# Five more seven-product pairs in the down projections, and earlier DMA sums, in a two-layer fp32 encoder on one core

## The chip, the cores and the metric

The kernel runs on one core of a Trainium2 chip. The metric is the time of one execution on the device in microseconds (us), and the median over several runs is compared. In the views of the profile PE is the tensor engine (PEld its weight loads), DVE the vector engine, ACT the scalar engine, POOL the GpSimd engine and SP the engine that issues most of the DMA transfers.

## The reference: what is computed

Two layers over 256 tokens of width 2048. Each layer has an input projection, a token mixer (differential attention in layer 0, windowed attention in layer 1) beside four memory heads, an output projection, and then an MLP with 8192 hidden features. Nearly all the work is matrix products with weights in fp32. The part that the change is about is this:

```python
x = x + heads @ w_out[i]
h = rms_norm(x, norm_mlp[i])
x = x + jnp.square(jax.nn.relu(h @ w_up[i])) @ w_down[i]
```

## The kernel before

**Numbers.** PE multiplies in a reduced fp32 format, so each fp32 operand is split into a high part and a rest: ACT copies the high part (`split`, line 439, operation CAST), DVE subtracts it to get the rest (line 440, TENSOR_TENSOR). A product is then three matmuls, hi x hi, lo x hi, hi x lo (`three`, lines 531 to 533). Weights come in pieces of 128x1024 fp32 (512 KB). SP issues the loads, at most a few pieces ahead of PE, since there are four buffers for `hi`, four for `lo`, and few for the raw pieces.

**Stages.** In each layer PE does, in this order: input projection ("in": 80 pieces in layer 0, 48 in layer 1), memory keys and values ("mem"), output projection ("out"), `up` (eight column groups of 16 pieces) and `down` (two halves of 32 pairs of pieces, each half 1024 of the 2048 output columns). In `up`, the finished hidden features are transposed on PE (line 1018), passed through relu and square on ACT (lines 1020 and 1021) and kept in `blk` tiles, some of them in DRAM (`hid`, line 1024). The transposes of the last group come when `down` has begun or is about to.

**Seven products instead of eight.** A pair of pieces is a 2 x 2 block problem with eight products, that is 24 matmuls of 512 columns. A "seven-product" or fast pair (`seven`, line 548) does it with seven products, 21 matmuls, in the manner of Strassen and Winograd: it needs sums of the weight blocks and differences of the hidden blocks. The sums are made by `sum_pair`: a first sum `a`, two further sums on DVE (lines 357 and 358), and the splits of `a` (parts `ah`, `al`) and of `b` (`bh`, `bl`). In the traces these four are tiles called `x` or `blk`, written from `big`. `FAST` names the fast pairs of a half of `down`, `LATE` those of layer 0's second half; `LATE_BLK` says which of these keep their sums in `blk`.

**First sums by DMA.** For a fast pair of `down` the first sum can be made in DRAM: POOL issues a copy (line 291) and then an accumulating copy (line 295) into a `madesum` tensor, which SP later loads instead of DVE adding. `make_sums` sets a list of moments, counted in pieces that PE's program has taken up: a first moment (`SUM_AT`), then one step every `SUM_GAP` pieces, or every `SUM_GAP_UP` pieces in `up`. What is left when `up` ends is issued at once (`while making`). Each step issues one addition and the next copy.

**Kept differences.** The hidden differences of a fast pair are made once in `up` (`keep`), split, stored to DRAM by POOL (`kept`, line 1000), and loaded again by POOL for each half, two pairs ahead (`load_kept`, line 1109, into `h2` tiles; there are six of these). Those of the last hidden features are made when `down` has begun.

**What sets the order.** Every engine takes its instructions strictly as the program has them. The order comes from the order of the calls, from `fetch`, which issues loads and splits two or three pieces ahead, and from small tasks that wait for a number of steps. `load_pair(..., early)` asks for a fast pair's raw pieces `LOOK` pairs ahead when enough of six big slots (five quads of the tile `big` and one `blk`) are free. The output projection does not do that before the change. Raw memory features are loaded when they are needed (`mem_part`).

Of the kernel before, what the change touches and what calls it, by code (L numbers as in the profile page):

```python
# [14 lines left out]
F32 = mybir.dt.float32  # L15
# [7 lines left out]
P = 128  # L23
S = 256
# [22 lines left out]
SINGLE = 4  # L47
AHEAD = 2
WARM = 10
FAST = (2, 4, 6, 8, 10, 12, 14, 16, 18, 20, 22, 24, 26, 28, 29)  # L50
LATE = (2, 4, 6, 8, 10, 12, 14, 16, 18, 20, 22, 24, 26, 28)
AWAY = range(6, 15)
LATE_BLK = (8, 12, 16, 20, 24, 28)
LOOK = 2
KEEP_AFTER = (2, 5, 8, 11)
SUM_AT = {0: 20, 1: 2}
SUM_GAP = 4
SUM_GAP_UP = 8
LAM_INIT = 0.8 - 0.6 * math.exp(-0.3 * 0)

G_ATTN, G_MEM, G_MLP = 0, 2 * KT, 4 * KT
# [9 lines left out]
def trunk(ctx: ExitStack, tc: tile.TileContext, xin, xtok, memin, memtok, posrel, gcol, rows,  # L71
# [19 lines left out]
    def quad(tag, shape=(P, 2, 2, 256), dt=F32R):  # L91
        return xp.tile(list(shape), dt, tag=tag, name=nm(tag), bufs={"x2": 8, "h2": 6, "blk": 10}[tag])
# [146 lines left out]
    def fast_pairs(name, h):  # L239

        if name.startswith("out"):
            return OUT_FAST[h]
        if name.startswith("up"):
            return UP_FAST[h]
        if name.startswith("down"):
            return LATE if (name, h) == ("down0", 1) else FAST
        return ()
# [37 lines left out]
    def make_sums(layer):  # L285

        name = f"down{layer}"

        def copy(h, j):
            made_in[name, h, j] = dp.tile([P, 2, 512], F32, name=nm("madesum"))  # L290
            after_piece(nc.gpsimd.dma_start(made_in[name, h, j].rearrange("p a n -> p (a n)"), weights[name][h, 2 * j]))

        def add(h, j):
            upper = weights[name][h, 2 * j + 1][:, 512:1024]
            nc.gpsimd.dma_start(made_in[name, h, j], upper.unsqueeze(1).broadcast_to([P, 2, 512]), accum_op=ALU.add)

        def after_piece(ins):
            tc.add_manual_dep(ins.ins, splits[0], mybir.DependencyInfo(mybir.DependencyClass.Sync, mybir.DependencyReason.DATA),
                              reason="behind a piece")

        def step(i):
            if i:
                add(*wanted[i - 1])
            if i < len(wanted):
                copy(*wanted[i])

        wanted = [(h, j) for h in range(2) for j in fast_pairs(name, h)]
        first, quiet, up = [at_piece[k, layer] for k in ("in", "mem", "up")]
        at = first + SUM_AT[layer]
        for i in range(len(wanted) + 1):  # L310
            making.append((at, lambda i=i: step(i)))
            at += SUM_GAP if at < quiet else SUM_GAP_UP
            at = max(at, up) if at >= quiet else at

    making = deque()
    fetched = [0]
# [11 lines left out]
    def load_pair(name, c, p, early=False):  # L328

        key = (name, c, p)  # L330
        if key in loaded or key in taken_raw or p not in fast_pairs(name, c) or early and len(slots) < (2 if name.startswith("up") else 4):
            return
        src = weights[name][c]
        taken = []
        first = raw_quad(name, (P, 1024), taken)
        nc.sync.dma_start(first, src[2 * p])
        if key in made_in:
            a = raw_quad(name, (P, 2, 512), taken)
            nc.sync.dma_start(a, made_in[key])
            raw = t2k([P, 512])  # L340
            nc.sync.dma_start(raw, src[2 * p + 1][:, 0:512])
        else:
            a = None
            raw = raw_quad(name, (P, 1024), taken)
            nc.sync.dma_start(raw, src[2 * p + 1])
        loaded[key] = first, raw, a, taken
# [23 lines left out]
    def fetch(parts=1, lead=None):  # L370

        name, c, j = plan.popleft()
        src = weights[name][c, j]
        p = j // 2
        seven_ = p in fast_pairs(name, c)
        down = name.startswith("down")
        if seven_:
            load_pair(name, c, p)
            raw = taken_raw[name, c, p][j % 2] if (name, c, p) in taken_raw else loaded[name, c, p][j % 2]
            if j % 2 == 0:  # L380
                taken_raw[name, c, p] = loaded[name, c, p][:2]
        else:
            raw = wp.tile([P, 1024], F32, tag="raw", name=nm("raw"))
        if name.startswith(("up", "down")) and j % 2 == 0:
            if down:
                load_hidden(p)
            for i in range(1, LOOK + 1):
                load_pair(name, c, p + i, True)
            if down:
                load_hidden(p + 1)  # L390
        hi = wp.tile([P, 1024], F32R, tag="hi", name=nm("hi"))
        lo = wp.tile([P, 1024], F32R, tag="lo", name=nm("lo"))
        n = 1024 // parts
        if seven_:
            with tc.issue_after(done[0].ins):
                if j % 2 == 0:
                    if down:
                        taken = sum_pair(name, c, p)
                    split(hi, lo, raw)
                else:  # L400
                    split(hi[:, 0:512], lo[:, 0:512], raw[:, 0:512])
                    if not down:
                        taken = sum_pair(name, c, p)
                    slots.extend(held_slots.pop(name, []) if down else taken)
                if down and j % 2 == 0:
                    held_slots[name] = taken
        else:
            for i in range(parts):
                s = slice(i * n, (i + 1) * n)
                if lead is not None:  # L410
                    lead(i)
                behind[0] = nc.sync.dma_start(raw[:, s], src[:, s])
                done[0] = split(hi[:, s], lo[:, s], raw[:, s])
                splits.append(done[0].ins.name)
        ready.append(((name, c, j), hi, lo))
# [64 lines left out]
    def chunk_tok(w, c, X2, before=None, lead=None, steps=1):  # L480
        ps = [bank("mm") for _ in range(2)]
        for j in range(8):
            if before is not None:
                before(j)
            hi, lo = piece(w, c, j, lead and (lambda i: lead(2 * j + i)))
            for kk in range(2):
                for t in range(2):
                    k = 2 * j + kk
                    ws = slice(kk * 512, kk * 512 + 512)
                    xh = X2[k][:, 0, t * P:(t + 1) * P]  # L490
                    xl = X2[k][:, 1, t * P:(t + 1) * P]
                    nc.tensor.matmul(ps[t], lhsT=xh, rhs=hi[:, ws], start=(k == 0), stop=False)  # L492
                    nc.tensor.matmul(ps[t], lhsT=xh, rhs=lo[:, ws], start=False, stop=False)  # L493
                    nc.tensor.matmul(ps[t], lhsT=xl, rhs=hi[:, ws], start=False, stop=(k == KT - 1))  # L494
            tick(steps)
        return ps
# [384 lines left out]
    def mem_stats():  # L881
# [22 lines left out]
                              parts[-1:], wait=MEM_AT, gap=0))  # L904
        Task([Light(means, 0)], parts)

    def mem_part(layer, qm, qd, H2):
        M2 = Halves()
        box = {}

        def before(j):
            if j % 2 == 0:
                raw = quad("h2", (P, 4, S), F32)
                nc.sync.dma_start(raw, memin[:, 512 * j:512 * j + 1024].rearrange("p (k s) -> p k s", s=S))
                box["raw"] = raw
            for k in (2 * j, 2 * j + 1):
                src = box["raw"][:, k % 4, :]
                make_x2(M2, k, src, gc[:, G_MEM + layer * KT + k:G_MEM + layer * KT + k + 1])

        ps = chunk_tok(f"mem{layer}", 0, M2, before)  # L920
        kT, kd = norm_T(ps, mst, 4, gc[:, G_MK + layer:G_MK + layer + 1], layer == 0)
        vbox = [None, None]
        heads = [plain_head(h, h, qm, kT, vbox, None, None, H2, 12 + h) for h in range(4)]
        firsts = [Task(h[:1], (qd, kd)) for h in heads]
        ps = chunk_tok(f"mem{layer}", 1, M2)
        flush([kd])
        vbox[0], vbox[1] = val_split(ps, mst)
        for i, h in enumerate(heads):
            done_heads[12 + i] = Task(h[1:], [firsts[i]])
# [256 lines left out]
    for g in range(3):  # L1186
# [20 lines left out]
        kT, kd = norm_T(ps, st0, 8, gc[:, G_AK:G_AK + 1])  # L1207
        for h in range(4):
            done_heads[4 * g + h] = Task(diff_head(h, qT, kT, v, bias, H2, 4 * g + h), [qd, kd] + rows_done)
    ps = chunk_tok("a", 9, X2)  # L1210
    qm, qd = norm_T(ps, st0, 4, gs[:, 2:3])
    mem_part(0, qm, qd, H2)
    X2 = out_proj(0, H2)
# [12 lines left out]
    for g in range(3):  # L1226
        ps = chunk_tok("b", g, X2)
        qT, qd = norm_T(ps, st1, 4, gs[:, 1:2])
        for h in range(4):
            n = 4 * g + h  # L1230
            done_heads[n] = Task(plain_head(h, n // 3, qT, kT, vv, bias, rw[:, R_SINK + n:R_SINK + n + 1], H2, n), [qd, kd])
    ps = chunk_tok("b", 5, X2)
    qm, qd = norm_T(ps, st1, 4, gs[:, 3:4])
    mem_part(1, qm, qd, H2)
    X2 = out_proj(1, H2)
# [70 lines left out]
```

## Time and profile before

| what | value |
|---|---|
| median of 3 runs (lowest, highest) | 2082.97 us (2082.69, 2083.38) |
| the profiled execution | 2082.35 us |
| its span | 2080.6 us |
| PE busy in the span | 2071.5 us |
| DVE busy | 1769.7 us (85%) |
| ACT busy | 1266.7 us (61%) |
| POOL busy | 182.1 us (9%) |
| moved by DMA | 563.62 MB, 271 GB/s on average |

On PE's clock of the trace, layer 0's `up` runs from 416 to 762 us, the halves of `down` from 762 to 929 and from 929 to 1096. In layer 1 `up` runs from 1396 to 1742, and `down` to 1913 and to 2081. A timeline row gives the start, the duration, the engine, the line, the operation with output and inputs, and in brackets the idle time before it with what ended it. A row of windows gives for each stretch the busy time of PE, PEld, DVE, ACT and POOL, then the granted PE clock (1.00 is full speed), the busy share of the DMA engines and what they moved. Matmuls overlap, so a matmul's listed duration is longer than the distance to the next.

### The profile page before, as it was taken

How to read it: one execution, taken by the hardware profiler on the slowest of the kernel's cores; microseconds unless marked ns; L12 is line 12 of the kernel's file. 1: busy time of each engine (PE TensorE's matmuls, PEld its weight loads, DVE VectorE, ACT ScalarE, POOL GpSimd, SP SyncE). 2: the span in 40 equal slices, each digit the busy share in tenths (PEclk: the TensorE clock that was granted, in tenths of full speed). 3: DMA queues.
4: the chain of work that ended last, by engine and by line, in shares of the span. 5: the costliest groups of instructions: out<-in, count | busy, mean ns of one | idle time of the engine just before them, and what ended most of it. 6: DMA issues, size and time to landing. Idle time of an engine off the chain costs nothing. (4 is left out here: it accounts for less than half of the span.)

```text
span 2080.6 us, 28646 instructions
## 1 busy us (share of the span) xinstructions
PE 2071.5 (100%) x10011; PEld 1720.7 (83%) x10011; DVE 1769.7 (85%) x2545; ACT 1266.7 (61%) x1892; POOL 182.1 (9%) x286
## 2 busy tenths in 40 slices
PE   9999999999999999999999999999999999999999
PEld 7878888888888888888888888888888887888887
DVE  7667778898999998898886677889999988989888
ACT  7467665566555666667655566566555665666664
POOL 1311100000011110000001100000001111000000
PEclk9999999999999999999999999999999999999999
DMA  8898864588899889988979975567789999998894
GB/s 319 298 297 273 270 204 158 188 257 242 266 292 295 262 287 333 335 282 285 332 259 291 269 233 194 172 211 239 251 276 292 295 280 338 323 334 311 289 334 167
DMA packets 168000, 563.62 MB, mean 271 GB/s; under 512 B 19456, under 2 KB 20480, under 8 KB 166656
## 3 DMA queue, kind: packets, MB, share of 16 engines
q1 hardware_dynamic: 132544, 439.62, 61.0%
q0 software_dynamic: 35168, 122.18, 21.8%
q8 instruction: 78, 1.28, 0.2%
q14 instruction: 66, 0.54, 0.1%
q10 hardware_dynamic: 144, 0.01, 0.0%
HBM read 531.19 MB, written 92.41 MB: 300 GB/s over the span
## 5 line engine op out<-in xcount | busy, mean ns | idle before, releaser
L439 ACT CAST hi<-raw 128x1024 fp32r<-128x1024 f32 (+1 forms) x522 | 525.6, 1036 | 443.6 <-issue 133.5
L440 DVE TENSOR_TENSOR lo<-raw,hi 128x1024 fp32r<-128x1024 f32 (+1 forms) x522 | 617.3, 1206 | 195.2 <-ACT hi L439 193.8
L492 PE MATMUL mm<-hi,x 128*128 128x512 f32 x640 | 255.8, 402 | 0.6 <-ACT hi L439 0.6
L493 PE MATMUL mm<-lo,x 128*128 128x512 f32 x640 | 250.7, 392 | 0.2 <-DVE lo L440 0.2
L494 PE MATMUL mm<-hi,x 128*128 128x512 f32 x640 | 250.2, 391 | 0.2 <-DVE x L436 0.2
L439 ACT CAST h<-big 128x1024 fp32r<-128x1024 f32 (+1 forms) x100 | 101.7, 1020 | 149.5 <-DVE big L283 130.8
L532 PE MATMUL mm<-lo,h 128*128 128x512 f32 (+1 forms) x461 | 179.2, 389 | 1.3 <-DVE lo L440 1.3
L531 PE MATMUL mm<-hi,h 128*128 128x512 f32 (+1 forms) x461 | 179.0, 389 | 1.4 <-ACT hi L439 1.4
L533 PE MATMUL mm<-hi,h 128*128 128x512 f32 (+1 forms) x461 | 178.9, 388 | 0.0
L532 PE MATMUL aux<-lo,h 128*128 128x512 f32 x442 | 172.2, 390 | 0.2 <-DVE lo L440 0.2
L531 PE MATMUL aux<-hi,h 128*128 128x512 f32 x442 | 172.2, 390 | 0.0
L533 PE MATMUL aux<-hi,h 128*128 128x512 f32 x442 | 172.0, 389 | 0.0
L531 PE MATMUL mm<-hi,x 128*128 128x512 f32 x414 | 161.7, 391 | 0.0
L533 PE MATMUL mm<-hi,x 128*128 128x512 f32 x414 | 161.1, 389 | 0.0
L532 PE MATMUL mm<-lo,x 128*128 128x512 f32 x414 | 161.1, 389 | 0.0
L531 PE MATMUL aux<-hi,x 128*128 128x512 f32 x398 | 155.5, 391 | 0.0
L532 PE MATMUL aux<-lo,x 128*128 128x512 f32 x398 | 154.9, 389 | 0.0
L533 PE MATMUL aux<-hi,x 128*128 128x512 f32 x398 | 154.6, 389 | 0.0
L440 DVE TENSOR_TENSOR lo<-big,hi 128x1024 fp32r<-128x1024 f32 (+1 forms) x141 | 144.3, 1043 | 0.0
L494 PEld LDWEIGHTS mm<-hi,x 128*128 128x128 f32 x640 | 120.1, 188 | 26.1 <-DVE x L436 0.5
L492 PEld LDWEIGHTS mm<-hi,x 128*128 128x128 f32 x640 | 120.4, 188 | 24.7 <-ACT hi L439 1.1
L493 PEld LDWEIGHTS mm<-lo,x 128*128 128x128 f32 x640 | 120.5, 188 | 23.2 <-DVE lo L440 1.2
(309 smaller groups left out, 4190.6 us busy)
## 6 DMA issues: line engine op xcount, KB each, us to landing
raw<-in_w_up SPq DMA_DIRECT2D x164, 512.0 KB, 6.3
raw<-in_w_down SPq DMA_DIRECT2D x138, 512.0 KB, 5.0
madesum<-in_w_down POOLq DMA_DIRECT2D x118, 512.0 KB, 6.7
big<-in_w_up SPq DMA_DIRECT2D x92, 512.0 KB, 4.3
raw<-in_w_a SPq DMA_DIRECT2D x72, 512.0 KB, 6.1
h<-kept POOLq DMA_DIRECT2D x59, 512.0 KB, 5.0
raw<-in_w_out SPq DMA_DIRECT2D x52, 512.0 KB, 4.0
big<-madesum SPq DMA_DIRECT2D x49, 512.0 KB, 5.5
```

The lines of the kernel that those rows point to most:

```text
L439: nc.scalar.copy(hi, src)
L440: return nc.vector.tensor_tensor(lo, src, as32(hi), op=ALU.subtract)
L492: nc.tensor.matmul(ps[t], lhsT=xh, rhs=hi[:, ws], start=(k == 0), stop=False)
L493: nc.tensor.matmul(ps[t], lhsT=xh, rhs=lo[:, ws], start=False, stop=False)
L494: nc.tensor.matmul(ps[t], lhsT=xl, rhs=hi[:, ws], start=False, stop=(k == KT - 1))
L531: nc.tensor.matmul(acc_, lhsT=x(0), rhs=w2[0][:, ws], start=first_, stop=False)
L532: nc.tensor.matmul(acc_, lhsT=x(0), rhs=w2[1][:, ws], start=False, stop=False)
L533: nc.tensor.matmul(acc_, lhsT=x(1), rhs=w2[0][:, ws], start=False, stop=last_)
```

## The change

1. `FAST` has 17 pairs instead of 15, and neighbours among them; `LATE` has 13 instead of 14. With three halves by `FAST` and one by `LATE` there are 64 fast pairs instead of 59. In the program PE has 15 instructions fewer, DVE 38 more rows, ACT 16, POOL 15.
2. Sums: layer 0 begins at piece 16 instead of 20. The steps go on every four pieces through "in", "mem" and "out", where before they paused from "mem" on until `up`. In `up` they come every 20 pieces (layer 0) or 12 (layer 1) instead of every 8. The first fast pair of each layer's first half has its first sum made by DVE.
3. Raw memory features are loaded one tile ahead, the first during the last chunk of the input projection. In the output projection a fast pair's raw pieces are asked for one pair ahead, without a limit on slots.

```diff
-FAST = (2, 4, 6, 8, 10, 12, 14, 16, 18, 20, 22, 24, 26, 28, 29)
-LATE = (2, 4, 6, 8, 10, 12, 14, 16, 18, 20, 22, 24, 26, 28)
+FAST = (2, 3, 5, 7, 8, 10, 12, 13, 15, 17, 18, 20, 22, 23, 25, 27, 29)
+LATE = (2, 5, 7, 8, 10, 12, 15, 17, 20, 22, 25, 27, 29)
 AWAY = range(6, 15)
-LATE_BLK = (8, 12, 16, 20, 24, 28)
+LATE_BLK = (8, 12, 17, 22, 27)
-SUM_AT = {0: 20, 1: 2}
+SUM_AT = {0: 16, 1: 2}
 SUM_GAP = 4
-SUM_GAP_UP = 8
+SUM_GAP_UP = {0: 20, 1: 12}
...
         wanted = [(h, j) for h in range(2) for j in fast_pairs(name, h)]
-        first, quiet, up = [at_piece[k, layer] for k in ("in", "mem", "up")]
-        at = first + SUM_AT[layer]
+        wanted.remove((0, fast_pairs(name, 0)[0]))
+        at = at_piece["in", layer] + SUM_AT[layer]
         for i in range(len(wanted) + 1):
             making.append((at, lambda i=i: step(i)))
-            at += SUM_GAP if at < quiet else SUM_GAP_UP
-            at = max(at, up) if at >= quiet else at
+            at += SUM_GAP if at < at_piece["up", layer] else SUM_GAP_UP[layer]
...
-        if key in loaded or key in taken_raw or p not in fast_pairs(name, c) or early and len(slots) < (2 if name.startswith("up") else 4):
+        if key in loaded or key in taken_raw or p not in fast_pairs(name, c) or early and len(slots) < {"o": 0, "u": 2, "d": 4}[name[0]]:
...
-        if name.startswith(("up", "down")) and j % 2 == 0:
+        if name.startswith(("out", "up", "down")) and j % 2 == 0:
             if down:
                 load_hidden(p)
-            for i in range(1, LOOK + 1):
+            for i in range(1, LOOK + 1 if not name.startswith("out") else 2):
                 load_pair(name, c, p + i, True)
...
+    mem_raw = {}
+
+    def load_mem(i):
+        mem_raw[i] = quad("h2", (P, 4, S), F32)
+        nc.sync.dma_start(mem_raw[i], memin[:, 1024 * i:1024 * i + 1024].rearrange("p (k s) -> p k s", s=S))
+
+    def mem_ahead(j):
+        if j == 5:
+            load_mem(0)
...
         def before(j):
             if j % 2 == 0:
-                raw = quad("h2", (P, 4, S), F32)
-                nc.sync.dma_start(raw, memin[:, 512 * j:512 * j + 1024].rearrange("p (k s) -> p k s", s=S))
-                box["raw"] = raw
+                if j:
+                    mem_raw.pop(j // 2 - 1)
+                if j < 6:
+                    load_mem(j // 2 + 1)
...
-    ps = chunk_tok("a", 9, X2)
+    ps = chunk_tok("a", 9, X2, mem_ahead)
...
-    ps = chunk_tok("b", 5, X2)
+    ps = chunk_tok("b", 5, X2, mem_ahead)
```

The change also moves instructions against each other, since pieces are asked for at other moments. Lines of `split` are numbered 439 before and 438 after, those of `three` 531 to 533 and 530 to 532. All rows below are from layer 1; layer 0 reads the same.

**First place: PE at the seam from `up` to `down`.** Before, the last matmuls of `up` (`x_13742` is an input feature tile) are followed at once by pair 0 of `down` (`h_16776` is the split hidden tile of that pair), and sixteen transposes of the last hidden features come after the pair's 24 matmuls:

```order
L531 MATMUL aux_16378<-hi_16678,x_13742 128x512
L532 MATMUL aux_16378<-lo_16679,x_13742 128x512
L533 MATMUL aux_16378<-hi_16678,x_13742 128x512
L531 MATMUL mm_16772<-hi_16725,h_16776 128x512
L532 MATMUL mm_16772<-lo_16726,h_16776 128x512
L533 MATMUL mm_16772<-hi_16725,h_16776 128x512
```

After, the transposes come first (two of the sixteen are shown before pair 0 here, and `h_16836` is now that pair's hidden tile):

```order
L1027 MATMUL aux_16910<-ident,t2k_16772 128x128
L1027 MATMUL aux_16910<-ident,t2k_16774 128x128
L530 MATMUL mm_16832<-hi_16792,h_16836 128x512
L531 MATMUL mm_16832<-lo_16793,h_16836 128x512
L530 MATMUL mm_16834<-hi_16798,h_16836 128x512
L531 MATMUL mm_16834<-lo_16799,h_16836 128x512
```

On ACT, before, the split of pair 0's hidden tile (first row) stands ahead of the last pieces of `up` (`hi_16678`, `hi_16684`), and pieces 2 and 3 of `down` (`hi_16780`, `hi_16791`) come only after the next hidden tiles:

```order
L439 CAST h_16776<-blk_14108 128x512
L439 CAST hi_16678<-raw_16677 128x1024
L439 CAST hi_16684<-raw_16683 128x1024
L566 COPY t2k_16710<-mm_16507 128x512
L439 CAST hi_16725<-raw_16720 128x1024
L439 CAST hi_16731<-raw_16730 128x1024
L439 CAST h_16785<-blk_14108 128x512
L439 CAST h_16871<-blk_14123 128x512
L439 CAST hi_16780<-raw_16779 128x1024
L439 CAST hi_16791<-raw_16790 128x1024
```

After, that split (`h_16836`) has pieces 2 and 3 (`hi_16844`, `hi_16855`) and the split of a kept difference (`h_16780`) ahead of it. `hi_16844` and `hi_16855` take the buffers of the last two pieces of `up` (`hi_16744`, `hi_16738`), which PE reads in its last six matmuls of `up`:

```order
L438 CAST hi_16738<-raw_16737 128x1024
L438 CAST hi_16744<-raw_16743 128x1024
L565 COPY t2k_16770<-mm_16570 128x512
L438 CAST hi_16792<-raw_16789 128x1024
L438 CAST hi_16798<-raw_16797 128x1024
L438 CAST hi_16844<-raw_16839 128x1024
L438 CAST hi_16855<-raw_16854 128x1024
L438 CAST h_16780<-t2k_16781 128x512
L438 CAST h_16836<-blk_14167 128x512
L438 CAST h_16849<-blk_14167 128x512
```

So the split that pair 0 needs has moved from before the end of `up` to behind it, and the transposes from behind pair 0 to ahead of it.

**Second place: ACT ahead of fast pair 5.** `h_17015` is the split of the last kept difference, number 29. `h_17167` is a hidden tile, number 7, that takes the same buffer again, so it waits until the store of that difference has landed. Behind it stands `x_17072`, the part `bh` of fast pair 5's sums:

```order
L438 CAST h_17015<-t2k_17016 128x512
L438 CAST h_17030<-blk_14546 128x512
L438 CAST hi_17066<-big_13725 128x1024
L438 CAST h_17080<-blk_14546 128x512
L438 CAST hi_17083<-t2k_16971 128x512
L438 CAST h_17121<-blk_14561 128x512
L438 CAST h_17167<-blk_14561 128x512
L438 CAST x_17072<-big_13725 128x1024
```

Before, the two hidden tiles that wait in this way (`h_16980` for difference 28, `h_17067` for difference 29) stand one pair earlier, among the splits for fast pair 4 (`x_16972` and its neighbours):

```order
L439 CAST h_16980<-blk_14481 128x512
L439 CAST h_17017<-blk_14481 128x512
L439 CAST x_16972<-big_13666 128x1024
L439 CAST h_17067<-blk_14496 128x512
L439 CAST x_17057<-big_13666 128x1024
```

So one such wait is left ahead of the pair, and it stands ahead of pair 5's second sum instead of beside pair 4's.

**Third place: POOL at the same seam.** Before, two copies and two additions of first sums stand around the first loads and stores of `down`:

```order
L1000 DMA kept_16632<-h_16625 128x1024
L291 DMA madesum_16737<-in_w_down 16x8192
L291 DMA madesum_16769<-in_w_down 16x8192
L1109 DMA h_16788<-kept_14308 128x1024
L295 DMA madesum_16737<-in_w_down 256x1x512
L295 DMA madesum_16769<-in_w_down 256x1x512
L1024 DMA hid_16828<-blk_16820 128x512
```

After, there are none, and the store of difference 29 (`kept_17022`) stands behind the load of the differences for fast pair 5 (`h_17033`):

```order
L1009 DMA kept_16614<-h_16607 128x1024
L1118 DMA h_16852<-kept_14367 128x1024
L1009 DMA kept_16787<-h_16780 128x1024
L1033 DMA hid_16892<-blk_16884 128x512
L1033 DMA hid_16901<-blk_16884 128x512
L1118 DMA h_16935<-kept_14462 128x1024
L1118 DMA h_17033<-kept_14668 128x1024
L1009 DMA kept_17022<-h_17015 128x1024
```

The four sum transfers have moved from this seam into earlier stages.

More of the change, by code (lines that the diff above doesn't have):

```diff
@@ L905, in mem_stats @@
         Task([Light(means, 0)], parts)
+    mem_raw = {}
[5 more added lines that the diff above has]
+            load_mem(0)
     def mem_part(layer, qm, qd, H2):
         M2 = Halves()
-        box = {}
         def before(j):
             if j % 2 == 0:
-                raw = quad("h2", (P, 4, S), F32)
-                nc.sync.dma_start(raw, memin[:, 512 * j:512 * j + 1024].rearrange("p (k s) -> p k s", s=S))
-                box["raw"] = raw
+                if j:
+                    mem_raw.pop(j // 2 - 1)
+                if j < 6:
+                    load_mem(j // 2 + 1)
             for k in (2 * j, 2 * j + 1):
-                src = box["raw"][:, k % 4, :]
+                src = mem_raw[j // 2][:, k % 4, :]
                 make_x2(M2, k, src, gc[:, G_MEM + layer * KT + k:G_MEM + layer * KT + k + 1])
```

## The prediction

> **What bounds the kernel now.** I read the page's busy shares first, then PE's waits, then PE's timeline where its step is not regular, then the windows.
>
> ```profile
> PE 2071.5 (100%) x10011; PEld 1720.7 (83%) x10011; DVE 1769.7 (85%) x2545; ACT 1266.7 (61%) x1892; POOL 182.1 (9%) x286
> PE mm L531 <- ACT hi L439: 1.4, 1, 1.4
> ```
>
> PE is busy for the whole span, and the largest entry among its waits is a single one of 1.4 us. So time goes down by fewer matmuls, and up by a wait that is new. What a matmul is worth is the distance between starts, not its listed duration, because they overlap:
>
> ```profile
> 1751.66 0.39 PE L533 MATMUL mm<-hi,h 128*128 128x512 f32 x1
> ...
> 1755.74 0.39 PE L533 MATMUL aux<-hi,h 128*128 128x512 f32 x1
> 1757.54 0.50 PE L531 MATMUL mm<-hi,h 128*128 128x512 f32 x1 [1.40 <-ACT hi L439]
> ...
> 1759.08 0.63 PE L532 MATMUL mm<-lo,h 128*128 128x512 f32 x1
> ...
> 1762.49 0.40 PE L531 MATMUL aux<-x,h 128*128 128x512 f32 x1
> ...
> 1770.02 0.39 PE L531 MATMUL mm<-hi,h 128*128 128x512 f32 x1
> 1771.01 0.50 PE L532 MATMUL mm<-lo,h 128*128 128x512 f32 x1 [0.59 <-DVE lo L440]
> ```
>
> From 1751.66 to 1755.74 there are 18 steps: 4.08 / 18 = 0.227 us each. From 1755.74 to 1762.49 there are 13, which should take 2.95 and took 6.75: 3.80 us lost at the start of layer 1's `down`. Of this 1.60 is not waiting: the eight steps from 1759.08 to 1762.49 take 3.41 instead of 1.81, and the windows show the granted clock down there:
>
> ```profile
> 1760.00:1765.00 5.00, 5.00 (x18) 3.98 (x17) 5.00 (x7) 3.35 (x5) 1.06 (x2) 0.75 1.09 397
> 1760.00:1780.00 20.00, 19.41 (x81) 15.57 (x80) 17.31 (x21) 13.53 (x19) 1.60 (x3) 0.94 1.02 379
> ```
>
> At 1771.01 another 0.99 - 0.227 = 0.76 is lost, so layer 1's start costs 4.56. Layer 0's start, and the start of its second half, lose less:
>
> ```profile
> 786.14 0.39 PE L531 MATMUL mm<-hi,h 128*128 128x512 f32 x1
> 787.01 0.50 PE L532 MATMUL mm<-lo,h 128*128 128x512 f32 x1 [0.48 <-DVE lo L440]
> 956.69 0.39 PE L531 MATMUL aux<-hi,h 128*128 128x512 f32 x1
> ...
> 958.49 0.40 PE L533 MATMUL aux<-hi,h 128*128 128x512 f32 x1
> ```
>
> The step from 786.14 took 0.87 instead of 0.23: 0.64. Five from 956.69 took 1.80 instead of 1.13: 0.67. These irregular places, 0.64 + 4.56 + 0.67 = 5.9 us, are what an edit of order can win or lose at `down`; everything else is matmul count.
>
> **The change part by part.**
>
> *Fewer matmuls.* The program has 15 PE instructions fewer, the three that a seventh product saves in each of five pairs. 15 x 0.227 = **-3.40 us**. This lies on the bound itself, so it is sure as long as PE is fed.
>
> *More splits and sums.* A fast pair costs DVE more. Its rows, and a stretch where fast and plain pairs alternate, and the end of the half, where pairs 28 and 29 are both fast:
>
> ```profile
> 785.13 1.23 DVE L440 TENSOR_TENSOR x<-big,x 128x1024 fp32r<-128x1024 f32 x1 [0.78 <-ACT x L439]
> 786.27 0.68 DVE L440 TENSOR_TENSOR lo<-t2k,hi 128x512 fp32r<-128x512 f32 x1
> 905.00:928.70 23.70, 23.70 (x106) 19.61 (x106) 23.70 (x31) 13.29 (x19) 0.53 (x1) 1.00 0.77 268
> 985.00:1035.00 50.00, 50.00 (x222) 41.39 (x221) 42.87 (x51) 31.57 (x40) 2.64 (x5) 1.00 0.97 328
> ```
>
> A wide operation follows the next after 1.14 (785.13 to 786.27), a half one, listed at 0.68, with the same overlap of 0.08 after 0.60. A plain pair needs two wide and one half, 2.9 us; a fast pair three wide (`lo` of the first piece, rests of `a` and `b`), four half (two sums, the half piece, the hidden tile): 5.8. PE takes 24 x 0.227 = 5.44 and 21 x 0.227 = 4.76. Alternating gives 8.7 of 10.2 us, 85%, and the row says 42.87 of 50, 86%. In the new list the densest stretch is pairs 12 to 23, eight fast and four plain: 8 x 5.8 + 4 x 2.9 = 58.0 of 59.8 us, 97%. The row from 905.00 shows DVE at 23.70 of 23.70 and PE too: a full DVE starves nobody for a while, though over 60 us little slack is left. I take 0 for DVE alone.
>
> *More transfers in that stretch.* Loads per pair, by the page's list:
>
> ```profile
> raw<-in_w_down SPq DMA_DIRECT2D x138, 512.0 KB, 5.0
> h<-kept POOLq DMA_DIRECT2D x59, 512.0 KB, 5.0
> big<-madesum SPq DMA_DIRECT2D x49, 512.0 KB, 5.5
> big<-in_w_down SPq DMA_DIRECT2D x49, 512.0 KB, 5.7
> t2k<-hid SPq DMA_DIRECT2D x72, 256.0 KB, 5.7
> t2k<-in_w_down SPq DMA_DIRECT2D x59, 256.0 KB, 5.9
> ```
>
> A fast pair loads 512 (piece) + 512 (sum) + 256 (half piece) + 512 (differences) KB and, from the twelfth pair on, 256 of hidden features: 2.10 MB; a plain pair 1.31. Alternating: 3.41 MB in 10.2 us, 334 GB/s against 328 in the row from 985.00. Pairs 12 to 23: 8 x 2.10 + 4 x 1.31 = 22.0 MB in 59.8 us, 368 GB/s. Bounds: nothing if the engines hold the 379 or 397 GB/s of the rows from 1760.00; (22.0 / 0.328) - 59.8 = 7.3 us a half if they stay at 328, 22 us over the three halves with this list. I take **+0.5**, near the lower end, since the demand lies below rates that the trace holds for 20 us.
>
> The Trainium skill (DMA: Bandwidth & Descriptors, "Where 436 GB/s comes from") says that for transfers between HBM and on-chip memory about 358 GB/s per core bind, not the fabric's 435. By that rule the stretch would take 22.0 / 0.358 = 61.5, an estimate of +1.7 a half and +5 in all. The trace differs over 20 us, with 379 GB/s.
>
> *Second half of layer 0.* There pair 4, ahead of the wait at 957, becomes plain: 2.9 us less work on DVE in front of it. **-0.65**, and 0 if the same wait comes at pair 5.
>
> *The seam from `up` to `down`.* Here order decides, twice in each layer. First, pair 0 waits for a hidden split that now stands behind pieces 2 and 3. Before, ACT ran these when PE had let go of `up`'s last buffers:
>
> ```profile
> 762.13 2.01 ACT L439 CAST hi<-raw 128x1024 fp32r<-128x1024 f32 x2 [4.49 <-PE aux L533]
> 768.06 1.91 PE L1018 MATMUL aux<-ident,t2k 128*128 128x128 f32 x16
> 769.72 0.48 PE L531 MATMUL mm<-hi,h 128*128 128x512 f32 x1
> 774.51 0.64 ACT L439 CAST h<-blk 128x512 fp32r<-128x512 f32 x1
> ```
>
> Two pieces to 764.1, then two half splits at some 0.55: pair 0's tile is ready at about 765.3, 2.9 us after `up`'s end (762.4). The transposes, now first, cover 769.72 - 768.06 = 1.7 to 2.0 of it. Left: **1.0** a layer (0.9 to 1.25).
>
> Second, pair 5. Counted from `up`'s end, pair 2 starts at 2.9 + 2 x 5.44 = 13.8 and pair 5 at 2.9 + 3 x 5.44 + 2 x 4.76 = 28.7; its second piece's rest is wanted four matmuls on, at 29.6. On ACT the split of difference 29 stands behind pieces 8 and 9, which want buffers that pair 2 frees after six and nine matmuls (15.1 and 15.8). With four wide ACT operations (0.95 each) and its own 0.5 it is done at 20.0, DVE's part at 21.0, and POOL sends the store at about 21.5 (pair 5's difference load, queued ahead of it, waits only for pair 2's end, 18). How long a store takes to land, by the page, by one case and by all transfers of `kept` tiles, loads among them:
>
> ```profile
> kept<-h POOLq DMA_DIRECT2D x30, 512.0 KB, 6.6
> 779.38 0.53 POOL L1000 DMA_DIRECT2D kept<-h  x1 [3.12 <-DVE h L440]
> 786.45 0.62 ACT L439 CAST h<-blk 128x512 fp32r<-128x512 f32 x1 [1.35 <-DMA kept<-h]
> DMA to landing us min/median/max: 3.7/5.8/9.1
> ```
>
> At 6.6 that is 28.1. Behind it come hidden tile 7 (0.6), the split of `b` (1.05), its rest (1.2) and the wanted rest (0.7): 31.7, so PE waits **2.0** (0 for a landing of 3.7, 4.6 for 9.1; 0 too if ACT is there a pair sooner). Queued behind the waiting tile on ACT are pair 5's and pair 7's sums, and DVE's rest waits for them. Third, a wait of 1.40 was followed by the half clock above, 1.60; one of 0.48 was not. For 2.0 I take half of it, **0.8** (0 to 1.6).
>
> The Trainium skill (TensorE: Matmul & The Clock Gate, "What's actually happening") has the clock fall only after an idle window of about 3.4 us. By it the third term is 0 and the sum lower by 1.6. The trace differs: the clock fell after 1.40 us idle, and stayed down for 3.41.
>
> New seams: 2 x (1.0 + 2.0 + 0.8) = 7.6. Old: 0.64 + 4.56 = 5.20. **+2.4**. I give nothing for the left-over sums that layer 1's seam loses: the store's landing is the bound there in both.
>
> *Sums in "mem" and "out".* They move from `up` to where the DMA engines have room:
>
> ```profile
> 300.00:400.00 100.00, 100.00 (x497) 84.39 (x496) 80.26 (x123) 57.59 (x101) 0.00 (x0) 1.00 0.54 173
> 455.00:530.00 75.00, 75.00 (x349) 62.60 (x348) 68.24 (x85) 45.62 (x59) 6.89 (x9) 1.00 0.84 256
> ```
>
> Twelve sums of two 512 KB transfers in layer 0's 147 us of "mem" and "out" add 86 GB/s to 173, the 256 that `up` bears with PE busy throughout. 0; earlier memory features and raw output pieces likewise, as PE loses nothing in that row. The first fast pair's own sum on DVE, 0.60, falls in the seam where DVE also waits: 0.
>
> Sum: -3.40 - 0.65 + 2.4 + 0.5 = **-1.15**, on the profiled 2082.35 (its span of 2080.6 and 1.75 around it, which I leave as they are): 2081.2. The median of the runs is 0.6 higher, so **2081.8**.
>
> **The rivals.** *A: seams nearly free.* If difference 29 is stored a pair sooner, no wait at pair 5 and no half clock: 2 x 1.0 - 5.20 = -3.2, and with the transfers at 0 the sum is -7.25: 2075.7. For it: layer 0 lost only 0.64 with the same store. Against: the split stands behind pieces 8 and 9. *B: seams at the high end*, 2 x (1.0 + 4.6 + 1.6) - 5.20 = +9.2, sum +5.65: 2088.6. For it: the transfers at 97% share; against: the median landing. *C, slower: transfers set the pace* in pairs 12 to 23. At 350 GB/s the stretch takes 62.9, +3.1 a half, +9.2 over three: 2081.8 - 0.5 + 9.2 = 2090.5. It decides once the engines give less than 368 there, and a DVE at 97% cannot catch up. For it: share 0.97 already at 328. Against: 379.
>
> **How the numbers follow.** This measurement tells 0.2%, 4.2 us, from no change: faster is below 2078.8, slower above 2087.1. Chances: forecast 0.49 (its own range 2077.5 to 2085, by waits at pair 5 of 0.5 to 3 us), A 0.27, B 0.08, C 0.16. Faster: A and a fifth of the forecast, 0.36. Slower: C but for its mild end, and B but for its, 0.19. Same: 0.45. Range 2075.5 to 2088.5: it holds A's value and the mild ends of B and C.
>
> **What would show it.** PE's rows 21 a fast pair, step 0.227. At both seams the first matmul of pair 0 waits about 1 us for ACT; the fourth or fifth matmul of pair 5 waits for DVE `lo`, whose chain goes back to a `kept` landing. No `madesum` row near 1740. At 929 to 979 no wait of PE. Wrong if PE runs through pair 5 (A), or shows waits on `lo` or on DMA in the middle of `down` with a share above 1.0 (C).

## The result, and the profile after

The changed kernel takes 2090.0 us (median of 7 runs, 2086.25 to 2092.9) and the kernel before 2083.38 (7 runs, 2081.46 to 2084.44). The ratio is 1.0031, with a 95% interval of 1.0019 to 1.0043: slower by 0.3%, where I had forecast a time within 0.2% of the old one, 2081.8, and a range up to 2088.5. The profiled execution has a span of 2088.2 us against 2080.6, so 7.6 us came in. In two of the versions below one execution of ten took several thousand us (10849 and 5395); the ratios leave these two out, and they move a median by less than 0.2 us.

The page of the changed kernel, and the larger entries of its view of PE's waits (what waited, for what, total us, how often, the longest):

```profile
PE 2071.3 (99%) x9996; PEld 1719.9 (82%) x9996; DVE 1789.2 (86%) x2583; ACT 1278.2 (61%) x1906; POOL 191.5 (9%) x301
PE mm L531 <- DVE lo L439: 6.6, 2, 3.6
PE aux L634 <- DVE t2k L674: 1.9, 1, 1.9
PE mm L530 <- ACT h L438: 1.3, 2, 0.7
PE mm L531 <- DVE blk L439: 1.1, 2, 0.6
PE aux L138 <- DVE ones L135: 1.1, 1, 1.1
PE aux L531 <- DVE h L439: 1.0, 1, 1.0
```

PE has fewer matmuls and yet the span is longer, so the loss is waiting, and matmuls at a lower clock behind some of the waits. The entry of line 138 stands before the change too. The first entry alone is 6.6 us in two pieces. PE's timeline shows them, one at the start of `down` in each layer, at the rest of pair 5's second piece:

```profile
764.62 1.93 PE L1027 MATMUL aux<-ident,t2k 128*128 128x128 f32 x16
767.22 0.50 PE L530 MATMUL mm<-hi,h 128*128 128x512 f32 x1 [0.67 <-ACT h L438]
...
793.87 0.39 PE L530 MATMUL mm<-hi,h 128*128 128x512 f32 x1
797.27 0.50 PE L531 MATMUL mm<-lo,h 128*128 128x512 f32 x1 [3.01 <-DVE lo L439]
...
1780.76 0.39 PE L530 MATMUL mm<-hi,h 128*128 128x512 f32 x1
1784.75 0.50 PE L531 MATMUL mm<-lo,h 128*128 128x512 f32 x1 [3.60 <-DVE lo L439]
1785.08 0.40 PE L532 MATMUL mm<-hi,h 128*128 128x512 f32 x1
1785.32 0.58 PE L530 MATMUL mm<-hi,h 128*128 128x512 f32 x1
...
1788.96 0.39 PE L530 MATMUL aux<-x,h 128*128 128x512 f32 x1
```

Less the regular step of 0.23, pair 5 costs 3.40 - 0.23 = 3.17 us in layer 0 and 3.99 - 0.23 = 3.76 in layer 1. The nine steps from 1785.32 to 1788.96 take 3.64 us instead of 2.04: half clock, 1.60 more. The row at 767.22 is the small wait at pair 0. What stands behind pair 5 is seen in three views of the same execution, the timelines of POOL, ACT and DVE in layer 0, and the first two in layer 1:

```profile
785.82 0.54 POOL L1009 DMA_DIRECT2D kept<-h  x1 [2.50 <-DVE h L439]
793.79 0.62 ACT L438 CAST h<-blk 128x512 fp32r<-128x512 f32 x1 [5.90 <-DMA kept<-h]
795.39 1.23 DVE L439 TENSOR_TENSOR x<-big,x 128x1024 fp32r<-128x1024 f32 x1 [4.05 <-ACT x L438]
...
1773.63 0.54 POOL L1009 DMA_DIRECT2D kept<-h  x1 [3.43 <-DVE h L439]
1781.27 0.62 ACT L438 CAST h<-blk 128x512 fp32r<-128x512 f32 x1 [5.63 <-DMA kept<-h]
```

POOL sends the store of difference 29 at 785.82. ACT's next hidden tile uses the same `h2` tile again and stands still for 5.90 us until the store has landed. Behind it on ACT is a part of pair 5's sums, on which DVE waits 4.05 us. Then PE waits. From POOL's issue to ACT's start it is 7.97 us in layer 0 and 7.64 in layer 1.

Three smaller losses are elsewhere. In layer 1's `up` (groups 4 and 5) two places wait in the same way (at the second, ACT waits 3.42 us for a `kept` landing), in layer 1's output part PE waits for sums of weight pieces, and in layer 0's input stage a transposition waits:

```profile
1593.29 1.14 POOL L1009 DMA_DIRECT2D kept<-h  x2 [2.37 <-DVE h L439]
1601.97 1.22 DVE L439 TENSOR_TENSOR h<-big,h 128x1024 fp32r<-128x1024 f32 x1 [2.92 <-ACT hi L438]
1603.25 0.50 PE L531 MATMUL aux<-h,blk 128*128 128x512 f32 x1 [0.97 <-DVE h L439]
...
1387.55 0.50 PE L531 MATMUL mm<-blk,blk 128*128 128x512 f32 x1 [0.51 <-DVE blk L439]
...
139.00 0.33 PE L634 MATMUL aux<-ident,t2k 128*128 128x128 f32 x1 [1.88 <-DVE t2k L674]
```

At 1593.29 the differences of the neighbours 12 and 13 are stored together (x2). DVE's operation at 1601.97 writes the tile that holds difference 12: that store lands 8.6 us after its issue, at 1601.9, and DVE starts at once. Its 2.92 us of idle time are put down to an ACT split that happened to end then, though it reads nothing of that split. In layer 0's `up` the same two stores land after 6.2 and 6.8 us, and PE loses nothing there. Fewer sums run beside them (a step every 20 pieces instead of 12), which may be the reason; no run isolates it.

The wait at 139.00 in the input stage is followed by a half clock too, from 140.13 to 143.54.

Adding for each matmul what it starts later than the regular step after the one before it, the changed kernel loses 36.2 us over its span and the old one 25.6, so 10.6 us more. Matmuls at half clock count as losses here. By place, in us:

| place | before | after |
|---|---|---|
| start of `down`, layers 0 and 1 together | 5.5 | 10.7 |
| second half of layer 0's `down` | 0.65 | 0 |
| layer 0's input stage, 100 to 150 us | 3.6 | 6.0 |
| layer 1's output part, second half | 0.1 | 2.1 |
| layer 1's `up`, 1600 to 1651 us | 0.1 | 2.9 |

### The profile page after: what moved, and what is told of

Its sections match the earlier page's. It is cut to its first block, busy times and chain, and to the rows that moved or that the text cites. A ratio compares the mean times of both kernels' runs of the same rounds, so it can differ in the third digit from the quotient of the medians.

```text
span 2088.2 us, 28792 instructions
## 1 busy us (share of the span) xinstructions
PE 2071.3 (99%) x9996; PEld 1719.9 (82%) x9996; DVE 1789.2 (86%) x2583; ACT 1278.2 (61%) x1906; POOL 191.5 (9%) x301
## 4 chain that ended last, share of the span: by engine, by line
PE 92%; issue 4%; DVE 2%; DMA 1%; ACT 1%; POOL 0%; POOLq 0%; DVEq 0%; ACTq 0%
PE mm L531 11%; PE mm L532 11%; PE mm L530 11%; PE aux L531 11%; PE aux L530 11%; PE aux L532 11%; PE mm L491 7%; PE mm L492 7%; PE mm L493 7%; DVE lo L439 1%; DMA kept<-h 1%; PE aux L634 1%; PE mm L1027 1%; PE aux L611 1%; PE aux L653 1%
## 5 line engine op out<-in xcount | busy, mean ns | idle before, releaser
L439 DVE TENSOR_TENSOR lo<-raw,hi 128x1024 fp32r<-128x1024 f32 (+1 forms) x512 | 606.8, 1205 | 182.2 <-ACT hi L438 181.1
L438 ACT CAST hi<-raw 128x1024 fp32r<-128x1024 f32 (+1 forms) x512 | 515.1, 1035 | 402.2 <-PE mm L493 114.6
L531 PE MATMUL mm<-lo,h 128*128 128x512 f32 (+1 forms) x438 | 170.3, 389 | 6.7 <-DVE lo L439 6.6
L530 PE MATMUL mm<-hi,h 128*128 128x512 f32 (+1 forms) x438 | 170.2, 389 | 1.3 <-ACT h L438 1.3
L532 PE MATMUL mm<-hi,h 128*128 128x512 f32 (+1 forms) x438 | 169.6, 388 | 0.0
L438 ACT CAST hi<-big 128x1024 fp32r<-128x1024 f32 (+1 forms) x147 | 129.9, 911 | 63.0 <-issue 54.8
L439 DVE TENSOR_TENSOR lo<-big,hi 128x1024 fp32r<-128x1024 f32 (+1 forms) x147 | 149.9, 1043 | 5.9 <-ACT hi L438 5.8
```

The lines of the kernel that those rows point to most:

```text
L438: nc.scalar.copy(hi, src)
L439: return nc.vector.tensor_tensor(lo, src, as32(hi), op=ALU.subtract)
L530: nc.tensor.matmul(acc_, lhsT=x(0), rhs=w2[0][:, ws], start=first_, stop=False)
L531: nc.tensor.matmul(acc_, lhsT=x(0), rhs=w2[1][:, ws], start=False, stop=False)
L532: nc.tensor.matmul(acc_, lhsT=x(1), rhs=w2[0][:, ws], start=False, stop=last_)
```

## The experiments

**Theory H:** the new waits come from `h2` tiles that a kept difference holds until its store has landed. The new list keeps more differences, some of them of neighbours. The rivals differ with each run.

### One tile more

```diff
-bufs={"x2": 8, "h2": 6, "blk": 10}[tag]
+bufs={"x2": 8, "h2": 7, "blk": 10}[tag]
...
-tag="t1k", name=nm("t1k"), bufs=4
+tag="t1k", name=nm("t1k"), bufs=2
-tag="sm", name=nm("sm"), bufs=36
+tag="sm", name=nm("sm"), bufs=24
...
-tag="h2", name=nm("xs"), bufs=6
+tag="h2", name=nm("xs"), bufs=7
```

> The changed kernel with seven instead of six h2 tiles (paid for by two instead of four t1k tiles and 24 instead of 36 small ones, which only the input stage uses much). Theory H: the new waits come from h2 tiles that a kept difference holds until its store has landed. With a seventh tile the next user comes one turn later. Then the waits of PE at pair 5 of both down starts (3.2 and 3.8 us, and the 1.5 us of half clock behind the second) and the two in layer 1's up (1601 and 1648, together 2.8) go: about 2090.0 - 8.5 - 2.8 = 2079, between 2077 and 2083 as the input stage may wait a little for its smaller tiles. Rival T: the transfers themselves are too many and everything lands late: the waits stay at PE whatever the tiles, 2088 to 2091.

Measured: 2080.14 us (10 runs, 2078.15 to 2082.71), ratio to the kernel before 0.9987 (0.9977 to 0.9996). PE's waits on rests, the DVE timeline at the place in `up`, and POOL and ACT at layer 1's start of `down`, with seven tiles:

```profile
PE mm L531 <- DVE lo L439: 0.4, 1, 0.4
...
1595.83 2.48 DVE L439 TENSOR_TENSOR h<-big,h 128x1024 fp32r<-128x1024 f32 x2
...
1769.38 0.54 POOL L1009 DMA_DIRECT2D kept<-h  x1 [8.13 <-DVE h L439]
1770.79 1.14 ACT L438 CAST h<-blk 128x512 fp32r<-128x512 f32 x2
```

The 6.6 us have become 0.4. In `up` the two rests of pair 4's sums run one behind the other (x2), where the second stood 2.92 us before. At 1770.79 ACT splits hidden tile 7 (the second of the two) without waiting, though the store of difference 29, sent at 1769.38, lands only at 1774.1. The time is within the range that theory H gave. The stores of difference 29 also landed sooner in this profile, after 5.4 and 4.7 us instead of 7.9 and 7.6, which alone would have shortened the waits; but ACT no longer waits for them at all. The waits need two things, a late landing and a next user too soon, and the second is what the change brought: at the same starts of `down` the four stores before the change took 7.0 to 7.8 us to land.

### The price of the seventh tile alone

```diff
-tag="t1k", name=nm("t1k"), bufs=4
+tag="t1k", name=nm("t1k"), bufs=2
-tag="sm", name=nm("sm"), bufs=36
+tag="sm", name=nm("sm"), bufs=24
```

> The changed kernel with its six h2 tiles, but with two t1k tiles and 24 small ones, the price that the seventh tile was paid with. Theory H: these tiles move nothing that waits, so the waits at pair 5 and in up are there: 2086 to 2092. Rival N: what the version with seven tiles gained came from the input stage's other tiles: 2079 to 2083.

Measured: 2091.59 us (5 runs, 2090.47 to 2092.54), ratio 1.0040 (1.0025 to 1.0054). Its waits on rests are the changed kernel's again, here with six tiles:

```profile
PE mm L531 <- DVE lo L439: 6.3, 2, 3.2
```

So the gain of the version above is that of the tile.

### The last difference sooner

```diff
-KEEP_AFTER = (2, 5, 8, 11)
+KEEP_AFTER = (2, 3, 8, 11)
```

> The changed kernel with KEEP_AFTER (2, 3, 8, 11) instead of (2, 5, 8, 11): the difference of every second hidden tile of a column group, number 29 among them, is made and split one pair earlier, and its store stands ahead of the load of pair 5's differences on GpSimd. Theory H: the store of 29 goes out some 3 us sooner, so the wait at pair 5 falls from 3.2 and 3.8 to 0 to 1 us, without the half clock: 2081 to 2084. Rival T: the landing moves little, 2088 to 2091.

Measured: median 2081.93 us of 10 runs, ratio 0.9992 (0.9982 to 1.0002). With the six tiles of the changed kernel, both waits at pair 5 are gone: the start of `down` loses 0.9 us in each layer. Layer 1's `up` still waits: 1.3 us at 1603 (1.1 in the changed kernel), less at 1649, and 1.0 at a new place, 1482. That again is theory H. Counted from pair 0's first matmul the store of difference 29 goes out after 13.1 us instead of 18.6 and 19.5. In this profile it also landed faster, after 5.3 and 5.8 us instead of 7.9 and 7.6; but with the old 7.9 it would have landed at 789.1 in layer 0, 0.2 us behind the moment at which ACT takes the tile again (788.89), so the sending alone removes nearly all of that wait.

### The lists alone, and everything but the lists

The kernel before, with the new `FAST`, `LATE` and `LATE_BLK` and nothing else:

> The kernel before with the new FAST, LATE and LATE_BLK alone (64 fast pairs; sums, memory features and output loads as before). Theory H: the lists alone bring the waits on h2 tiles, at pair 5 and in up, more of them since up carries more sums here: 2088 to 2094. Rival S: the sums in memory and output parts and the earlier loads are what costs: 2080 to 2084 here.

Measured: 2105.64 us (4 runs, 2104.17 to 2106.03), ratio 1.0107 (1.0092 to 1.0122). Both theories were too low. PE and POOL at layer 1's start of `down`:

```profile
1763.38 0.39 PE L533 MATMUL mm<-hi,h 128*128 128x512 f32 x1
1784.39 0.79 PE L531 MATMUL mm<-hi,h 128*128 128x512 f32 x1 [20.62 <-DMA h<-kept]
...
1749.29 1.52 POOL L291 DMA_DIRECT2D madesum<-in_w_down  x2
1751.67 0.57 POOL L1000 DMA_DIRECT2D kept<-h  x1 [0.86 <-DVE h L440]
1766.05 1.11 POOL L295 DMA_DIRECT2D madesum<-in_w_down  x1 [13.81 <-DMA madesum<-in_w_down]
1767.59 1.05 POOL L295 DMA_DIRECT2D madesum<-in_w_down  x1 [0.42 <-DMA madesum<-in_w_down]
1768.17 0.99 POOL L291 DMA_DIRECT2D madesum<-in_w_down  x1
1768.68 1.09 POOL L1109 DMA_DIRECT2D h<-kept  x1
```

With 64 pairs and the old schedule many sums are left when `up` ends. They are issued at once, each addition waits for its copy to land (13.81 us here), and the load of differences for pair 2, the first fast pair, stands behind them on POOL until 1768.68. Sent beside all these transfers, it takes another 15.7 us to land, and PE waits 20.62 us. So the new schedule is needed for the new lists: in this respect the change does what its parts need. Of the places that theory H named, `up` does wait with the lists alone: 4.8 us are lost in layer 0 instead of 0.7, half clock included, and 2.7 in layer 1 instead of 0.7. In layer 0, where sums run every 8 pieces here, ACT waits 4.58 us for a store that lands after 9.7. Layer 0's pair 5 does not wait (its start of `down` loses 1.7 us), so that wait takes the lists and the rest of the change together; in layer 1 it can't be judged behind the 20.62 us.

The changed kernel with the old lists:

> The changed kernel with the old FAST, LATE and LATE_BLK (59 fast pairs; new times of the sums, new loads of memory features and output pieces). Theory H: no new wait in up or at pair 5; the 2.0 us in layer 1's output part stay; the left-over sums at 1740 are gone, so layer 1's start may lose less than 4.6: 2080 to 2085. Rival S: 2087 to 2091.

Measured: 2083.96 us (10 runs), ratio 1.0006 (0.9996 to 1.0015), within what theory H gave. Its start of `down` loses 1.7 and 2.5 us, and the waits in `up` are absent, but layer 1's output part loses 1.6. Without the new lists the schedule and the loads gain nothing and cost nothing measurable.

### The output part: sums or loads

The version with seven tiles, with the old loads of memory features and output pieces:

```diff
-len(slots) < {"o": 0, "u": 2, "d": 4}[name[0]]
+len(slots) < (2 if name.startswith("up") else 4)
-        if name.startswith(("out", "up", "down")) and j % 2 == 0:
+        if name.startswith(("up", "down")) and j % 2 == 0:
...
-                if j < 6:
-                    load_mem(j // 2 + 1)
+                load_mem(j // 2)
...
```

> The changed kernel with seven h2 tiles, and the loads of memory features and output pieces as before the change (asked for when needed). Theory M: in layer 1's output part it is the sums of down's first terms, three of them in flight with pieces that land after 9 to 12 us instead of 4 to 5, that make PE wait there (2.0 to 2.9 us at 1371 to 1388). Then the wait stays, at 1.5 to 4 us, and the time is 2080 to 2083. Rival L: it is the earlier, bunched output loads: the wait goes, 2077 to 2079.

Measured: 2087.79 us (10 runs), ratio 1.0022 (1.0012 to 1.0032), slower than either theory said. The output part of layer 1 loses 3.3 us, that of layer 0 now 4.0, and the starts of `down` 2.4 to 2.7. So rival L is out: with the sums there, the output part gets worse in both layers without the earlier loads. Memory features and output pieces were changed back together, so which of the two helps isn't told. Why the starts of `down` also lose more was not followed up.

No sums in layer 1's output part, again with seven tiles:

```diff
-            at += SUM_GAP if at < at_piece["up", layer] else SUM_GAP_UP[layer]
+            at += SUM_GAP - layer if at < at_piece["up", layer] else SUM_GAP_UP[layer]
+            if layer and at_piece["out", 1] <= at < at_piece["up", 1]:
+                at = at_piece["up", 1]
...
-SUM_GAP_UP = {0: 20, 1: 12}
+SUM_GAP_UP = {0: 20, 1: 9}
```

> The changed kernel with seven h2 tiles, and in layer 1 no step of the sums in the output part: every 3 pieces in input and memory parts, then every 9 pieces in up. Theory M: the output part's pieces land in 4 to 5 us again and the 2.9 us at 1371 to 1388 go: 2076.5 to 2079; up carries three sums more and, with the seventh tile, does not wait. Rival L: the wait in the output part stays at 2 to 3 us: 2080 to 2083.

Measured: median 2081.34 us of 10 runs, ratio 0.9994 (0.9984 to 1.0004). In its profile the output part loses 0.1 us where the version with seven tiles lost 2.9, as theory M says. The time did not follow, and lies in the range of rival L: its memory part lost 2.2 instead of 0.5 and its `up` 1.6 more, where the sums went instead. The transfers show what the sums do. The rows are from the list of DMA issues in twenty microseconds of layer 1's output part (how many, KB each, median us to landing), and the same stretch as a window; first the kernel before (1352 to 1372), then the changed one (1355 to 1375), then the version without sums there:

```profile
raw<-in_w_out SPq DMA_DIRECT2D x6, 512.0 KB, 4.6
1352.00:1372.00 20.00, 20.00 (x98) 16.78 (x98) 16.15 (x22) 14.27 (x25) 0.00 (x0) 1.00 0.72 235
```

```profile
raw<-in_w_out SPq DMA_DIRECT2D x6, 512.0 KB, 9.9
madesum<-in_w_down POOLq DMA_DIRECT2D x5, 512.0 KB, 10.0
1355.00:1375.00 20.00, 20.00 (x98) 16.80 (x97) 13.54 (x19) 12.07 (x23) 4.15 (x5) 1.00 1.02 363
```

```profile
raw<-in_w_out SPq DMA_DIRECT2D x6, 512.0 KB, 5.3
```

Five transfers of sums in 20 us take the busy share from 0.72 to 1.02, and the pieces that PE needs land after 9.9 us instead of 4.6; without them it is 5.3. The version with seven tiles had 10.5 us there and lost 2.9; the one with the small tiles alone had the same sums, a landing of 8.7, and lost 0.1. So the sums make the landings late, and in these profiles PE waited behind landings of 9.9 and 10.5 us and not behind one of 8.7. With the same sums the wait is not the same each time.

### The input stage, and a version that beats both

With seven tiles, layer 0's sums from piece 20 on:

```diff
-SUM_AT = {0: 16, 1: 2}
+SUM_AT = {0: 20, 1: 2}
```

> The changed kernel with seven h2 tiles, and layer 0's sums begun at piece 20 instead of 16. Theory A: the loss of 1.7 to 2.1 us at 137 us in layer 0's input stage comes with the earlier sums, since the runs with piece 20 (the kernel before, and its version with the new lists) lose 0.4 to 1.1 there: the loss falls by about 1.2, 2078 to 2080. Rival V: it varies from run to run and does not follow the sums: 2080, and the loss at 137 stays near 1.7.

Measured: 2079.09 us (10 runs, 2077.71 to 2080.29), ratio 0.9980 (0.9970 to 0.9989). The stretch from 100 to 150 us loses 2.7 us instead of 5.1. Over all nine profiles of experiments the six that begin at piece 16 lose 4.2 to 6.0 there and the three that begin at 20 lose 2.6 to 3.5, so theory A holds for the place. In the time the step is not resolved: the intervals of the ratios with piece 16 and with piece 20 overlap.

On top of that, half as many sums in layer 1's output part:

```diff
-SUM_GAP_UP = {0: 20, 1: 12}
+SUM_GAP_UP = {0: 20, 1: 10}
...
-            at += SUM_GAP if at < at_piece["up", layer] else SUM_GAP_UP[layer]
+            at += SUM_GAP_UP[layer] if at >= at_piece["up", layer] else 8 if layer and at >= at_piece["out", 1] else SUM_GAP
```

> The changed kernel with seven h2 tiles, layer 0's sums from piece 20, and in layer 1's output part a step every 8 pieces instead of 4 (then every 10 instead of 12 in up). Theory M: half as many sums beside the output pieces, so the 2.0 us at 1371 to 1388 fall below 1: 2077 to 2079. Rival L: they stay, or come back in up: 2079 to 2081.

Measured: 2078.05 us (10 runs, 2076.14 to 2081.03), ratio 0.9975 (0.9966 to 0.9985). It is the fastest version here, 5.4 us under the kernel before. The output part's loss went from 2.0 to 0.1, while `up` lost 2.2 instead of 0.2 and the second start of `down` 2.2 more. In the one profile the sum of losses is therefore no smaller than without this edit, and the intervals of the two overlap: it is not shown to be faster than the version before it.

## Why the prediction was wrong

The forecast was -1.15 us. The profiled executions differ by +7.6, so the sum was 8.8 us too low. Four steps failed. The seams, taken at +2.4, came out at +5.2 (10.7 less 5.5), because the landing of a store was taken too short: 2.8 too little. The sums in the output part were put at 0 and cost 2.0 in layer 1. Layer 1's `up` (+2.8) and layer 0's input stage (+2.4) had no term at all. These four make 10.0. Against them, the transfers cost nothing instead of 0.5, the rest of the kernel lost some 1.1 us less than before, and the matmuls brought 3.0 instead of 3.4. All of these are readings of one execution on each side.

**Fewer matmuls, -3.40:** the page counts 15 PE instructions fewer. The losses grew by 10.6 us and the span by 7.6, which leaves -3.0 for the matmuls. With a seventh tile the changed kernel comes out below the old one, as it must if this term is real. No run isolates it.

**Second half of layer 0, -0.65:** right. The wait at 957 is gone.

**Denser pairs: DVE 0, transfers +0.5, rival C:** the time is near the 2090.5 of rival C, but not through its mechanism. In the changed kernel the densest stretches of layers 0 and 1 look like this:

```profile
830.00:895.00 65.00, 65.00 (x289) 53.83 (x288) 61.23 (x72) 45.29 (x55) 4.22 (x8) 1.00 0.98 353
1810.00:1880.00 70.00, 70.00 (x310) 57.98 (x310) 64.86 (x75) 48.77 (x60) 4.22 (x8) 1.00 0.96 340
```

PE is busy for all of the 65 and 70 us, with DVE at 94% and 93% and the transfers at 353 and 340 GB/s. PE waits for nothing there. Had only the total been read, C would have passed for right.

**The seam, +2.4:** the right place and mechanism, and the size too small. Pair 0's wait came as worked out (0.67 by the row, 0.83 against the step, for 1.0). At pair 5 the time that POOL sends the store was met closely: 785.82 is 21.2 us after `up`'s end (764.6), worked out as 21.5. So was what follows the landing: from ACT's start to PE's it is 3.48 us (793.79 to 797.27), worked out as 3.6. The term that was mis-sized is the landing: I took the median of 6.6 us over the whole execution, and the two stores took 8.0 and 7.6 from their issue to ACT's start. In layer 1 the store also went out 0.9 us later, 22.1 us after `up`'s end. The waits became 3.17 and 3.76 instead of 2.0, both within the given 0 to 4.6, and the half clock came once here, at 1.60, which is what 0.8 twice makes. All told the starts of `down` lose 10.7 where I had 7.6 (and 5.5, not 5.2, before). The time of a store had to be taken from the same crowded stretch. The four stores at the two seams before took 7.0 to 7.8 us, and one of them, 779.38 to 786.45, stands in the rows that I showed. With their mean of 7.2 the sum gives a wait of 2.6, so a part of the miss stays open. The nothing for the left-over sums was not safe either: with the old lists and the new schedule layer 1's start lost 2.5 us instead of 4.7, 1.6 of the difference being the half clock that did not come.

**"Sums in mem and out: 0":** wrong. I set the mean rate, 173 + 86 = 259 GB/s, against a stretch of `up` that bears 256, and the mean did come out: the same window of the changed kernel shows 249 GB/s, with PE busy throughout:

```profile
300.00:400.00 100.00, 100.00 (x497) 84.33 (x497) 81.42 (x129) 57.73 (x100) 12.41 (x16) 1.00 0.82 249
```
But the sums come in bursts beside bursts of pieces: the twenty microseconds shown above have a share of 1.02 within a mean of 0.82 to 0.85 over the part. It cost 2.0 us in layer 1 in this execution and nothing in layer 0, where I can't say why.

**Not in the sum at all:** neighbours in the list give `up` a third difference to keep in some groups, and stores sent together that hold two of its six tiles: 2.8 us in layer 1. I had looked for DVE time there, and not for who has the tile next. The same rule that I applied to the seam, a tile is free when its store has landed, was not applied to `up`. And in the profiles layer 0's input stage loses about 2 us more with the earlier beginning at piece 16, which I did not price; a part of it here is the half clock behind the wait at 139.00. Why the transposition there comes later was not followed up.

**Rival A** is what the version with seven tiles shows: with both starts of `down` nearly free and no waits in `up`, 2080.1, not 2075.7, as the output part and the input stage keep their losses. **Rival B** came near in the total, 2088.6 for 2090.0, but not by its mechanism: it has 14.4 us at the starts of `down`, where 10.7 were lost.

## What to carry to other kernels

A tile that is stored is in use until the store has landed, so a change that stores more often, or two at once, must be checked for who takes that tile next and what stands behind that user on its engine; one more tile can be worth more than the work that the change saves. Price a transfer on a critical chain by its landing time in the same stretch, not by the median, and price added transfers by how they fall beside the others, not by the mean rate. A forecast whose time is met by another rival's mechanism is not met: look at the place.

## What the runs showed of the hardware

The half clock follows steps of 3.41 us, and not the length of a wait. In the eleven traces of this document the granted clock falls only at a whole number of such steps after it first rose. Before the change it rose at 4.61 us and fell at 1759.06, which is 514 steps of 3.413; after it, it rose at 7.01 and fell at 140.13 and 1785.35, 39 and 521 steps later. It came back one step later when PE was busy again. The rows below are cut at these steps (behind a row's length stands PE's busy time; the granted clock stands before the last two numbers); first two of the kernel before, then five of the changed one:

```profile
1755.65:1759.06 3.41, 1.78 (x7) 0.92 (x6) 2.32 (x7) 3.41 (x7) 0.80 (x2) 1.00 1.03 390
1759.06:1762.47 3.41, 3.41 (x9) 2.65 (x8) 3.32 (x5) 3.41 (x5) 0.54 (x1) 0.50 1.06 410
```

```profile
792.08:795.49 3.41, 2.18 (x10) 1.48 (x8) 0.10 (x1) 1.70 (x3) 0.53 (x1) 1.00 1.08 416
795.49:798.91 3.42, 1.64 (x7) 1.36 (x8) 3.42 (x5) 3.42 (x4) 0.00 (x0) 1.00 0.92 310
798.91:802.32 3.41, 3.41 (x17) 2.80 (x16) 3.41 (x4) 2.01 (x4) 0.00 (x0) 1.00 0.83 270
1781.94:1785.35 3.41, 0.60 (x3) 0.52 (x4) 2.48 (x4) 3.41 (x4) 0.00 (x0) 1.00 0.93 294
1785.35:1788.76 3.41, 3.41 (x10) 2.64 (x9) 3.41 (x5) 1.89 (x3) 0.00 (x0) 0.50 0.77 255
```

The wait of 1.40 us at 1757 fell within one step, which was idle for 1.63 us, and the next step ran at half clock. The wait of 3.01 us at 797 was spread over two steps, idle for 1.23 and 1.78, and the clock stayed up. At 1785 one step was idle for 2.81, and it fell. Over all eleven traces, with the clock up, no step with up to 1.58 us idle was followed by a half clock, and every step with 1.84 or more was; from 1.63 to 1.78 it went both ways. So a wait of about 2 us costs 1.6 us more or nothing, by where it falls. What I took, half of 1.6 for each such wait, was the right kind of guess: in the changed kernel it came once in two, and in the version with the small tiles alone, with waits of the same kind, twice in two.

The Trainium skill (TensorE: Matmul & The Clock Gate, "What's actually happening") says that the window over which activity is judged is 3413 ns long and runs freely, without starting anew when the kernel starts. The steps here fit that. They do not fit its table's condition for the half clock, at least one idle window of about 3.4 us: 1.63 us of idle time within a step was enough at 1757.

A 512 KB piece landed after 4.6 us (the median of six) at a busy share of 0.72 before the change, and after 9.9 at 1.02 after it, in the same stage, though the bytes moved rose only from 235 to 363 GB/s.
